# Hybrid decoder layer on one core: turned blocks ahead of the next weights, gates and position table off TensorE

## The chip, the core and the metric

The kernel runs on one core of a Trainium2 chip. Times are device microseconds of one launch. A core has TensorE (PE, with its weight loads as PEld), VectorE (DVE), ScalarE (ACT), GpSimd (POOL) and SyncE (SP), each with its own instruction queue, worked off in order. Here SP issues nearly all DMA transfers. Engines wait for one another by semaphores.

## What is computed

One decoder layer for 256 positions of width 1024, in float32. A combined projection feeds an mLSTM branch (4 heads of 256), an attention branch (8 heads of 128 with a T5 table of relative positions) and two gates; both branches are projected, gated, added and projected again, and a gated MLP with a short convolution follows. Each half ends in a LayerNorm.

```python
def hybrid_mixer(x, w_in, b_in, conv_qk, mlstm_norm, rel_bias, w_branch_a, w_branch_b, w_out):
    proj = jnp.einsum("bsd,dn->bsn", x, w_in) + b_in
    q_m, k_m, v_m, o_m, i_m, f_m, q_b, k_b, v_b, g_a, g_b = _split_cols(proj, SPLIT_SIZES)
    qk = jax.nn.silu(causal_dwconv(jnp.concatenate([q_m, k_m], axis=-1), conv_qk))
    ...
    h_m = mlstm_chunkwise(...)            # i_m, f_m: 4 gates each per position
    y_a = sigmoid(o_m) * head_norm(h_m, mlstm_norm)
    h_b = moba_attention(..., rel_bias)   # 256 positions are one block: plain causal softmax
    merged = sigmoid(g_a) * (y_a @ w_branch_a) + sigmoid(g_b) * (y_b @ w_branch_b)
    return merged @ w_out

x = layer_norm(ALPHA * x + hybrid_mixer(x), ln1_g, ln1_b)
x = layer_norm(ALPHA * x + conv_gated_mlp(x), ln2_g, ln2_b)
```

## The kernel before, in words

All weights stream from HBM in chunks of 1 MB (128 x 2048 floats), in the order that `chunk_order` gives. Each matmul of the reference is three matmuls: every operand is split into a high and a low part (`split_into`, L92 to L95: ScalarE casts to `wh`, VectorE subtracts to `wl`), and high x high, low x high and high x low are summed in PSUM (`mm3`). So a chunk is 48 matmuls on TensorE, and beside it a split of 2048 columns on ScalarE and VectorE, and one transfer on SP.

The order on each engine is the order in which the program is written. The loop over chunks `s` in `run` does, for each: `elem_work(s)`, the element work that waited for the chunk before (`evac`), side work (`side_elem`) and in between the split of chunk s+2; then `load(s + 5)`, a transfer into one of three `raw` buffers, which waits until VectorE has split the chunk that was there; then the chunk's matmuls and side work of TensorE (`side_pe`). `self.mixed[s]` is a function that sets the order of the element work of one step.

The first 32 chunks after the first four come in 4 groups of 8 (qm, qb, km, kb, vm, vb, ga, gb). A group holds one mLSTM head and two attention heads. Beside its chunks run its scores (pss, psl), softmax weights (`lg`), the mLSTM output (psn, then `yt`) and the product of softmax weights and values (pso); `b` is the group's first chunk, and the offsets below count from it. Softmax weights and `yt` have to be turned (transposed) for the products that follow. Groups 0 to 2 do it without TensorE: VectorE turns blocks of 32x32 (`turn`, L658), SP writes them to HBM (`turn_out`, L663, tile `flip`) and reads them back in four transfers (`turn_in`, L671), each read after the write has landed. Write and reads of a block stand in steps of their own, behind the weights of the step before:

```python
self.mixed[b + 7] = lambda w: [lambda: out(0), ...] + w + [..., lambda: dve_t(1)]
self.mixed[b + 8] = lambda w: [lambda: back(0), lambda: out(1), el_n2] + w + [dve_y]
wrap(9, lambda w: [lambda: back(1), lambda: out(2)] + w + [lambda: el_t(0)])
wrap(10, lambda w: [lambda: back(2), lambda: el_t(1)] + w)
```

`el_t` splits the turned softmax weights into `pth`, `ptl`, `ptf`; `el_y` and `el_o` make the halves `yah`, `yal` and `ybh`, `ybl` of the branch inputs. The last group turns on TensorE against an identity (pst for softmax weights, psy for `yt`). After the groups come the branch chunks wa (which read yah, yal) and wb (ybh, ybl), in the order wa, wb, wa, wb, ..., then wo, and the MLP.

TensorE also makes three small things at the start: the table of relative positions (ps_rel, a one-hot product, L567), the turn of the input and forget gates from positions on partitions to positions in a row (ps_gt, L596), where VectorE scans along them, and the turn back of two results (ps_gc, L634).

Of the kernel before, what the change touches and what calls it, by code (L numbers as in the profile page):

```python
# [18 lines left out]
P = 128  # L19
# [25 lines left out]
def chunk_order():  # L45
# [4 lines left out]
    for c in range(4):  # L50
        order += [("wa", c), ("wb", c)]
# [21 lines left out]
class Kernel:  # L73
# [106 lines left out]
    def run(self):  # L180
# [32 lines left out]
        rel = xp.tile([2 * NB, 8], F32, name="rel")  # L213
        onehot = xp.tile([2 * NB, S], F32, name="onehot")
# [39 lines left out]
        twice = (2, NB)  # L254
        small = [(vec, self.vec_d), (ident, self.ident_d)]
        for t, d in ((rel, self.rel_d.unsqueeze(0).to_broadcast([*twice, 8])),
                     (onehot, self.onehot_d[:, 0:S].unsqueeze(0).to_broadcast([*twice, S]))):
            small.append((t, d))
# [21 lines left out]
        both = xp.tile([2 * NB, 8], F32R, name="relhl")  # L280
        oneh = self.ybl.rearrange("p k s -> p (k s)")[0:2 * NB, 0:S]

        def rel_split():
            nc.scalar.copy(both, rel)
            nc.scalar.copy(oneh, onehot)
            nc.vector.tensor_sub(both[NB:], rel[NB:], both[NB:].bitcast(F32))
        self.step_o(whl, bo)
        for s in range(4, 9):
            if s == 7:
                self.split(4)  # L290
            self.load(s)
            if s < 6:
                for _ in range(2):
                    dma(*small.pop(0))
# [36 lines left out]
        self.rel_bias_expand(both, oneh, rel_split)  # L331
        self.gates_schedule(bif)
        for gi in range(NG):
            self.group_schedule(gi)

# [3 lines left out]
                      for i, (m, n) in enumerate(((1, 3), (1, 3), (2, 2)))] for g in range(NG - 1)]  # L339
# [7 lines left out]
        for f in [self.gate_sums] + self.o_sums:  # L347
            f()
        self.split(5)
        for s, (kind, i) in list(enumerate(self.order))[4:]:  # L350
# [3 lines left out]
            if s == first["wa"]:  # L354
# [21 lines left out]
            self.elem_work(s, [] if late else self.split_parts(s + 2))  # L376
# [184 lines left out]
    def rel_bias_expand(self, rel, onehot, split):  # L561
        nc = self.nc
        st = {}

        def pe():
            st["ps"] = ps = self.ps_side([8, S], "ps_rel")
            nc.tensor.matmul(ps, rel, onehot, start=True, stop=True)  # L567

        def elem():
            ev = self.xp.tile([8, LTOE], F32, name="ev")  # L570
            nc.vector.tensor_scalar(ev[:, P:LTOE], self.backward(st["ps"]), 1.0 / ATT_SCALE, None, op0=ALU.mult)
            nc.vector.memset(ev[:, 0:P], NEG)
            nc.gpsimd.dma_start(self.table, ev)
            self.load_band(0)
        self.side_elem.setdefault(4, []).append(split)
        self.mixed[4] = lambda w: w[-1:] + w[:-1]
        self.side_pe.setdefault(4, []).append(pe)
        self.side_elem.setdefault(5, []).append(elem)


    def gates_schedule(self, bif):
        nc, mp = self.nc, self.xp
        st = {}
        v = nc.vector

        def e0():
            gt = mp.tile([P, 2, 8], F32, name="gt")
            for t in range(2):
                v.tensor_add(gt[:, t, :], self.psg[t][:, 256:264], bif)
            st["gt"] = gt  # L590

        def p0():
            ps = self.ps_side([4, 2, S], "ps_gt")
            for w in range(2):
                for t in range(2):
                    nc.tensor.transpose(ps[:, w, t * P:(t + 1) * P], st["gt"][:, t, 4 * w:4 * w + 4], self.ident)  # L596
            st["ps"] = ps

        def e1():
            ps = st["ps"]  # L600
            big = mp.tile([P, KT, S], F32, tag="xraw", name="gates")
            fs, t1, F, G, M, nFM, nM = (big[0:4, k, :] for k in range(7))
            v.tensor_copy(fs, ps[:, 1, :])
            v.scalar_tensor_tensor(t1, fs, -1.0, fs, op0=ALU.mult, op1=ALU.min)
            st["g"] = fs, t1, F, G, M, nFM, nM
# [6 lines left out]
        def e1b():  # L612
            fs, t1, F, G, M, nFM, nM = st["g"]
# [4 lines left out]
        def e1c():  # L618
            fs, t1, F, G, M, nFM, nM = st["g"]
            v.tensor_sub(G, st["ps"][:, 0, :], F)  # L620
            v.tensor_tensor_scan(M, self.ones4[:, S:2 * S], G, 0.0, op0=ALU.max, op1=ALU.max)

        def e1d():
            fs, t1, F, G, M, nFM, nM = st["g"]
            v.tensor_scalar(self.nM[0:4, :], M, -1.0, None, op0=ALU.mult)
            v.scalar_tensor_tensor(nFM, F, -1.0, M, op0=ALU.mult, op1=ALU.subtract)
            st.update(G=G, nFM=nFM)
            nc.sync.dma_start(self.mrows, self.nM[0:4, :])

        def p1():  # L630
            ps = self.ps_side([P, 2, 2, 4], "ps_gc")
            for w, n in enumerate(("G", "nFM")):
                for t in range(2):
                    nc.tensor.transpose(ps[:, w, t, :], st[n][:, t * P:(t + 1) * P], self.ident[0:4, 0:4])  # L634
            st["gc"] = ps

        def e2():
            self.gcol = self.const.tile([P, 2, 4], F32, name="gcol")
            self.floor = self.const.tile([P, 2, 4], F32, name="floor")
            nc.scalar.copy(self.gcol, st["gc"][:, 0])  # L640
            self.floor_exp = lambda: nc.scalar.activation(self.floor, st["gc"][:, 1], AF.Exp)
# [3 lines left out]
        self.side_pe.setdefault(b, []).append(p0)  # L645
# [733 lines left out]
```

## Time and profile before

| | us |
|---|---|
| three runs | 481.77, 482.19, 483.7; median 482.19 |
| the profiled execution: its time, its span | 483.66, 482.0 |
| TensorE, VectorE, ScalarE, POOL busy | 473.4, 368.1, 309.9, 18.8 |
| mean granted clock of TensorE | 0.997 |
| bytes moved by DMA | 96.64 MB, mean 201 GB/s |

In the rows below, L148 is line 148 of the kernel; `out<-in` names the tiles; in a timeline the first number is the start from the span's beginning, the second the duration, both in us, and brackets tell the idle time of the engine ahead of the instruction and what ended it. Matmuls overlap: what one costs is the distance from its start to the next start, not its duration.

### The profile page before, as it was taken

The numbers are of one execution on the slowest core, as the hardware profiler recorded it, in microseconds if no ns is written. First come the engines' busy times: TensorE is split into PE (matmuls) and PEld (weight loads), VectorE is DVE, ScalarE is ACT, GpSimd is POOL, SyncE is SP. The second block draws the span as 40 slices with busy tenths as digits, with TensorE's granted clock in tenths as the row PEclk, the third lists the DMA queues.
The fourth block names the chain that finished last, engine by engine and source line by source line (L and its number), as shares of the span: only waits on it lengthen the run. The fifth ranks groups of instructions, "written<-read, shape, count | busy, mean of one in ns | idle before, by whom it ended". The sixth has DMA issues, their size and how long they took to land.

```text
span 482.0 us, 9466 instructions
## 1 busy us (share of the span) xinstructions
PE 473.4 (98%) x3803; PEld 457.1 (95%) x3803; DVE 368.1 (76%) x647; ACT 309.9 (64%) x543; POOL 18.8 (4%) x42
## 2 busy tenths in 40 slices
PE   8999999999999999999999999999999999999994
PEld 5999999999999999998999999999999999999984
DVE  4887978787768786885766798988768767768876
ACT  5679777777768775977754622767456544556871
POOL 0301001000100010001000001000000000000000
PEclk9999999999999999999999999999999999999998
DMA  7995647754875477544944490827454555456202
GB/s 231 317 333 152 251 176 237 241 191 175 247 234 187 175 244 237 186 176 165 354 181 175 175 349 37 307 97 262 176 195 169 221 201 182 175 194 227 99 0 89
DMA packets 27387, 96.64 MB, mean 201 GB/s; under 512 B 9201, under 2 KB 14013, under 8 KB 18125
## 3 DMA queue, kind: packets, MB, share of 16 engines
q1 hardware_dynamic: 26110, 91.79, 54.2%
q0 software_dynamic: 1232, 4.24, 2.8%
q8 instruction: 30, 0.49, 0.4%
q14 instruction: 15, 0.12, 0.1%
HBM read 92.99 MB, written 3.03 MB: 199 GB/s over the span
## 4 chain that ended last, share of the span: by engine, by line
PE 89%; ACT 4%; DVE 4%; DMA 1%; issue 0%; SPq 0%; DVEq 0%; ACTq 0%
PE ps_up L148 25%; PE ffn L148 13%; PE ps_wb L148 5%; PE mix L148 5%; PE ps_qb L148 5%; PE ps_qm L148 5%; PE ps_km L148 4%; PE ps_wa L148 4%; PE ps_ga L148 3%; PE ps_kb L148 3%; PE ps_vm L148 3%; PE ps_gb L148 3%; PE ps_vb L148 3%; DVE wl L95 2%; ACT wh L94 2%; PE ps_o0a L436 1%
## 5 line engine op out<-in xcount | busy, mean ns | idle before, releaser
L95 DVE TENSOR_TENSOR wl<-raw,wh 128x1024 fp32r<-128x1024 f32 (+4 forms) x147 | 180.2, 1263 | 30.3 <-ACT wh L94 26.6
L94 ACT CAST wh<-raw 128x1024 fp32r<-128x1024 f32 (+4 forms) x147 | 151.9, 1079 | 8.3 <-DMA raw<-in_wst_dram 4.5
L148 PE MATMUL ps_up<-x1h,wl 128*128 128x256 f32 x320 | 88.5, 276 | 0.0
L148 PE MATMUL ps_up<-x1h,wh 128*128 128x256 f32 x320 | 88.4, 276 | 0.0
L148 PE MATMUL ps_up<-x1l,wh 128*128 128x256 f32 x320 | 88.4, 276 | 0.0
L148 PEld LDWEIGHTS ps_up<-x1l,wh 128*128 128x128 f32 x320 | 60.1, 188 | 0.4
L148 PEld LDWEIGHTS ps_up<-x1h,wh 128*128 128x128 f32 x320 | 60.1, 188 | 0.3
L148 PEld LDWEIGHTS ps_up<-x1h,wl 128*128 128x128 f32 x320 | 60.1, 188 | 0.0
L1150 DVE SCALAR_TENSOR_TENSOR cu<-ps_up,vec,cu 128x255 f32<-128x255 f32 (+1 forms) x80 | 33.0, 475 | 20.1 <-ACT cu L1146 20.1
L148 PE MATMUL ffn<-wh,hl 128*128 128x512 f32 (+2 forms) x94 | 35.5, 378 | 0.0
L148 PE MATMUL ffn<-wl,hh 128*128 128x512 f32 (+2 forms) x94 | 35.4, 377 | 0.0
L148 PE MATMUL ffn<-wh,hh 128*128 128x512 f32 (+2 forms) x94 | 35.3, 375 | 0.0
L94 ACT CAST hh<-cu 128x256 fp32r<-128x256 f32 x22 | 8.9, 407 | 40.4 <-DVE cu L1161 40.4
L1146 ACT ACTIVATE cu<-ps_up,vec 128x256 f32<-128x256 f32 x40 | 16.7, 469 | 22.0 <-PE ps_up L148 22.0
L148 PEld LDWEIGHTS ffn<-wh,hl 128*128 128x128 f32 x94 | 17.7, 188 | 3.2
L148 PEld LDWEIGHTS ffn<-wl,hh 128*128 128x128 f32 x94 | 17.7, 188 | 3.1
L148 PEld LDWEIGHTS ffn<-wh,hh 128*128 128x128 f32 x94 | 17.7, 188 | 3.0
L148 PE MATMUL ps_wa<-yal,wh 128*128 128x256 f32 x64 | 18.2, 284 | 0.5 <-DVE yal L803 0.4
L148 PE MATMUL ps_wa<-yah,wh 128*128 128x256 f32 x64 | 18.2, 284 | 0.0
L148 PE MATMUL ps_wb<-ybh,wh 128*128 128x256 f32 x64 | 18.0, 281 | 0.0
L148 PE MATMUL ps_wb<-ybl,wh 128*128 128x256 f32 x64 | 18.0, 281 | 0.0
L148 PE MATMUL ps_wb<-ybh,wl 128*128 128x256 f32 x64 | 18.0, 281 | 0.0
(354 smaller groups left out, 1444.9 us busy)
## 6 DMA issues: line engine op xcount, KB each, us to landing
raw<-in_wst_dram SPq DMA_DIRECT2D x72, 1024.0 KB, 4.9
raw<-in_wst_dram SPq DMA_DIRECT2D x10, 512.0 KB, 6.4
raw<-in_wst_dram SPq DMA_DIRECT2D x8, 256.0 KB, 4.8
lnrow<-in_rows_dram POOLq DMA_DIRECT2D x4, 512.0 KB, 7.0
flip<-turn SPq DMA_DIRECT2D x6, 192.0 KB, 4.4
lg<-flip SPq DMA_DIRECT2D x24, 48.0 KB, 5.2
xraw<-in_xt_dram SPq DMA_DIRECT2D x8, 128.0 KB, 2.6
toe<-table POOLq DMA_DIRECT2D x4, 256.0 KB, 3.9
```

The lines of the kernel that those rows point to most:

```text
L94: self.nc.scalar.copy(wh, raw)
L95: self.nc.vector.tensor_sub(wl, raw, wh.bitcast(F32))
L148: self.nc.tensor.matmul(ps, a[i], b[i], start=start and i == 0, stop=stop and i == 2)
L436: mm(ps[t], x[:, k, t * P:(t + 1) * P], w, start=start and k == 0, stop=stop and k == KT - 1)
L1146: act.activation(cu[:, j, :], ps[:, j, :], AF.Copy, scale=tap(2, j))
L1150: v.scalar_tensor_tensor(cu[:, j, o:], ps[:, j, :S - o], tap(t, j), cu[:, j, o:], op0=ALU.mult, op1=ALU.add)
```

## The change

It has five parts.

1. Write and reads of a turned block are issued together, in the step in which VectorE turns it (`turn` now holds all three), so on SP they stand ahead of that step's weights, and the reads ahead of the next weights. `el_t` comes two steps after the turn, and pso, `el_o` and `el_y` one step earlier than before.
2. The last group's softmax weights go the same way instead of over TensorE; its `yt` still goes over TensorE (psy). Its pso comes after the first wa chunk; `el_y` stands at the head of its step, with half of a weight split (`self.kept`) behind it.
3. The branch chunks come by pairs: wa, wa, wb, wb.
4. The gates are turned by VectorE (32x32 blocks) and put in place by POOL copies; results go back the same way. The exponential of `floor` is taken in place.
5. The table of relative positions is written by POOL, bucket by bucket, from 8 rows; the one-hot input is no longer loaded. One product per group for `scl` moves to POOL.

TensorE at the first chunk of the first group (qm, and after it qb), before:

```order
L148 MATMUL ps_qm_455<-xtl,wh_371 128x256
L148 MATMUL ps_qm_455<-xth,wl_372 128x256
L567 MATMUL ps_rel<-ybl,relhl 8x256
L596 MATMUL ps_gt<-ident,gt 4x128 x4
L148 MATMUL ps_qb_544<-xth,wh_436 128x256
L148 MATMUL ps_qb_544<-xtl,wh_436 128x256
```

and now:

```order
L148 MATMUL ps_qm_479<-xtl,wh_368 128x256
L148 MATMUL ps_qm_479<-xth,wl_369 128x256
L148 MATMUL ps_qb_554<-xth,wh_463 128x256
L148 MATMUL ps_qb_554<-xtl,wh_463 128x256
L148 MATMUL ps_qb_554<-xth,wl_464 128x256
```

The five small matmuls are gone; ps_gc and the six of pst go in the same way.

SP from the second block of the first group on (raw: weights; lg, yt: turned blocks that come back), before:

```order
L671 DMA lg_901<-flip_420 32x4x96 x4
L663 DMA flip_421<-turn 128x384
L89 DMA raw_1106<-in_wst_dram 128x2048
L671 DMA lg_997<-flip_421 32x4x96 x4
L663 DMA flip_422<-turn 128x2x256
L89 DMA raw_1184<-in_wst_dram 128x2048
L671 DMA yt_1008<-flip_422 32x8x64 x4
L89 DMA raw_1254<-in_wst_dram 128x2048
```

and now:

```order
L644 DMA flip_418<-turn 128x384
L648 DMA lg_1010<-flip_418 32x4x96 x4
L89 DMA raw_1055<-in_wst_dram 128x2048
L644 DMA flip_419<-turn 128x2x256
L648 DMA yt_1021<-flip_419 32x8x64 x4
L89 DMA raw_1127<-in_wst_dram 128x2048
L89 DMA raw_1200<-in_wst_dram 128x2048
```

A block's reads stood one transfer of weights behind its write; now they follow it, and SP waits for the write's landing in front of the weights.

ScalarE from the last group's turned weights to the first wa chunk, before:

```order
L94 CAST pth_886<-pst_0_2941 128x256
L863 COPY ptf_888<-pst_0_2941 128x128
L771 ACTIVATE yt_2863<-yt_2863,scl_2862 128x256 x2
L94 CAST pth_889<-pst_1_2945 128x256
L863 COPY ptf_891<-pst_1_2945 128x128
L551 ACTIVATE sga<-ps_ga_2892,vec 128x256 x2
L94 CAST wh_2949<-raw_2688 128x1024 x2
L551 ACTIVATE sgb<-ps_gb_2968,vec 128x256 x2
L802 ACTIVATE yah<-psy_3017,vec 128x256 x2
L883 ACTIVATE ybh<-pso_3022,vec 128x256 x2
```

and now:

```order
L743 ACTIVATE yt_2879<-yt_2879,scl_2878 128x256 x2
L94 CAST pth_898<-lg_2770 128x256
L815 COPY ptf_900<-lg_2770 128x128
L542 ACTIVATE sga<-ps_ga_2916,vec 128x256 x2
L94 CAST wh_2965<-raw_2697 128x1024
L765 ACTIVATE yah<-psy_3027,vec 128x256 x2
L94 CAST wh_2965<-raw_2697 128x1024
L94 CAST pth_901<-lg_2868 128x256
L815 COPY ptf_903<-lg_2868 128x128
L542 ACTIVATE sgb<-ps_gb_2978,vec 128x256 x2
```

The yah pair moved ahead of one cast and of sgb; the second turned block moved behind it.

```diff
 def chunk_order():
...
-    for c in range(4):
-        order += [("wa", c), ("wb", c)]
+    for c in (0, 2):
+        order += [("wa", c), ("wa", c + 1), ("wb", c), ("wb", c + 1)]
...
-            if s == first["wa"]:
+            if s == first["wa"] + 1:
                 self.elem_work(s)
...
+            parts = [] if late else self.split_parts(s + 2)
+            if s == first["wa"] - 1:
+                self.kept, parts = parts[-1], parts[:-1]
+            self.elem_work(s, parts)
             self.load(s + 5)
...
+    def rel_bias_expand(self, rel):
+        g = self.nc.gpsimd
+        ev = self.xp.tile([8, LTOE], F32, name="ev")
+        g.memset(ev[:, 0:P], NEG)
+        bucket = _buckets(np.arange(S))
+        one = int(np.argmax(bucket[1:] == bucket[:-1]))
+        runs = [(0, one, 0)]
+        for b in range(one, NB):
+            d = np.flatnonzero(bucket == b)
+            runs.append((int(d[0]), int(d[-1]) + 1, b))
+        for lo, hi, b in runs:
+            src = rel[:, b:b + 1].to_broadcast([8, hi - lo]) if lo else rel[:, 0:hi]
+            g.tensor_scalar(ev[:, P + lo:P + hi], src, 1.0 / ATT_SCALE, None, op0=ALU.mult)
+        g.dma_start(self.table, ev)
+        self.load_band(0)
...
         def e0():
-            gt = mp.tile([P, 2, 8], F32, name="gt")
+            big = mp.tile([P, KT, S], F32, tag="xraw", name="gates")
+            g.memset(big[:, 7, :], 0.0)
+            g.memset(big[0:32, 0:6:5, :], 0.0)
+            gt, gx = big[:, 7, 0:P], big[:, 7, P:2 * P]
...
+            v.transpose(gx, gt)
+            for j in range(4):
+                src = gx[32 * j:32 * j + 4, :].rearrange("p (t w c) -> p w t c", t=2, w=2)
+                dst = big[0:4, 0:4:3, :].rearrange("p w (t j c) -> p w t j c", t=2, j=4)[:, :, :, j, :]
+                g.tensor_copy(dst, src)
-        def p0():
...
-                    nc.tensor.transpose(ps[:, w, t * P:(t + 1) * P], st["gt"][:, t, 4 * w:4 * w + 4], self.ident)
...
-        def p1():
...
+        def e1e():
+            big = st["big"]
+            for w, k in enumerate((0, 5)):
+                v.transpose(big[0:32, 1 + w, :], big[0:32, k, :])
+            cols = self.const.tile([P, 2, 2, 4], F32, name="gcol")
+            for j in range(4):
+                src = big[0:32, 1:3, :].rearrange("p w (t j c) -> p w t j c", t=2, j=4)[:, :, :, j, 0:4]
+                g.tensor_copy(cols[32 * j:32 * j + 32], src)
...
+    def turn(self, t, d):
+        m, _, f = d.shape
+        n, w = t.shape[1], t.shape[1] // m
+        tmp = self.ap.tile([P, 4 * P], F32, tag="turn", name="turn", bufs=2)[:, 0:n * P]
+        for k in range(m):
+            self.nc.vector.transpose(tmp[:, k * f:(k + 1) * f].rearrange("p (b c i) -> p c b i", b=4, i=32),
+                                     t[:, k * w:(k + 1) * w].rearrange("p c (b i) -> p c b i", b=4))
+        self.nc.sync.dma_start(d.rearrange("m p f -> p m f"), tmp.rearrange("p (m f) -> p m f", m=m))
         t = t.rearrange("p c s -> p (c s)").rearrange("p (k f) -> p k f", k=4 * m)
         for b in range(4):
             src = d[:, :, b * (f // 4):(b + 1) * (f // 4)].rearrange("m (a j) f -> j m a f", a=4)
             self.nc.sync.dma_start(t[32 * b:32 * b + 32], src.rearrange("j m a f -> j (m a) f"))
...
             nc.gpsimd.tensor_tensor(scl, scl, self.mhalf, op=ALU.pow)
+            nc.gpsimd.tensor_tensor(scl, scl, den, op=ALU.mult)
...
         def el_n2():
-            v.tensor_mul(scl, scl, st["den"])
...
-        if flip:
...
-        at(self.side_pe, 6, lambda: pe_t(0))
-        at(self.side_pe, 6, lambda: pe_t(1))
...
-        self.mixed[b + 7] = lambda w: [lambda: el_t(0), el_n2, lambda: el_t(1)] + w
...
+        at(self.side_elem, 5 + o, lambda: turn(0))
+        self.mixed[b + 6 + o] = lambda w: ([lambda: el_l(1), lambda: el_e(1), el_n1] + w
+                                           + [lambda: el_l2(1), el_n1b, lambda: turn(1)])
+        if last:
+            self.mixed[b + 7] = lambda w: [el_n2, lambda: el_t(0)] + w
+            at(self.side_pe, 7, pe_y)
+            self.mixed[b + 8] = lambda w: [el_y, self.kept, lambda: el_t(1)] + w
+        else:
+            self.mixed[b + 8] = lambda w: [el_n2, lambda: el_t(0), lambda: turn(2)] + w
+            self.mixed[b + 9] = lambda w: w[0:1] + [lambda: el_t(1)] + w[1:]
+            at(self.side_elem, 10, el_y)
+        at(self.side_pe, 8 + o, pe_o)
+        at(self.side_elem, 9 + o, el_o)
```

More of the change, by code (lines that the diff above doesn't have):

```diff
@@ L253, in run @@
         nc.gpsimd.partition_broadcast(self.bvm, brow[:, D:2 * D])
[L254 to L258, printed above, removed]
+        small = [(vec, self.vec_d), (ident, self.ident_d), (rel, self.rel_d.rearrange("b h -> h b"))]
         v3 = [t.rearrange("p (k f) -> p k f", k=KT) for t in whl[3]]
@@ L292, in run @@
             if s < 6:
-                for _ in range(2):
+                for _ in range(2 if s == 4 else 1):
                     dma(*small.pop(0))
@@ L346, in run @@
         first = {k: self.order.index((k, 0)) for k in ("wa", "wo", "up")}
[L347 removed]
+        for f in self.o_sums:
             f()
@@ L558, in step_gb @@
         self.step_gate(s, "gb", g, V_BGB)
[L561 to L578, printed above, removed]
+    def rel_bias_expand(self, rel):
[13 more added lines that the diff above has]
+        self.load_band(0)
     def gates_schedule(self, bif):
@@ L628, in e1d @@
             nc.sync.dma_start(self.mrows, self.nM[0:4, :])
-        def p1():
[L631 to L641, printed above, removed]
+        def e1e():
[6 more added lines that the diff above has]
+                g.tensor_copy(cols[32 * j:32 * j + 32], src)
+            self.gcol = cols[:, 0]
+            self.floor = cols[:, 1]
+            self.floor_exp = lambda: nc.scalar.activation(self.floor, self.floor, AF.Exp)
@@ L671, in turn_in @@
             self.nc.sync.dma_start(t[32 * b:32 * b + 32], src.rearrange("j m a f -> j (m a) f"))
-    def turned(self, t):
-        return t.rearrange("p c s -> p (c s)").rearrange("p (a c i) -> p c a i", a=4, i=32)
     def group_schedule(self, g):
@@ L680, in group_schedule @@
         b = self.start_g[g]
-        flip = g < NG - 1
+        last = g == NG - 1
         def row_m():
@@ L845, in el_l2 @@
                 a.activation(o, o, AF.Copy, scale=sm[:, t:t + 1])
-        def pe_t(i):
-            ps = self.ps_side([P, 3, P], f"pst{g}_{i}")
-            for k in range(3):
-                nc.tensor.transpose(ps[:, k, :], st["p", i][:, k, :], self.ident)
-            st["t", i] = ps
-        def el_t(i):
-            th, tl, tf = self.pt[i]
-            if flip:
-                ps = self.turned(st["p", i])
-                th, tl, tf = (t.rearrange("p c (a i) -> p c a i", a=4) for t in (th, tl, tf.unsqueeze(1)))
-                self.split_into(th, tl, ps[:, 0:2])
-                a.copy(tf, ps[:, 2:3])
-                return
-            ps = st["t", i]
-            self.split_into(th, tl, ps[:, 0:2, :])
-            a.copy(tf, ps[:, 2, :])
+        def el_t(i):
+            ps = st["p", i].rearrange("p c s -> p (c s)").rearrange("p (a c i) -> p c a i", a=4, i=32)
+            th, tl, tf = (t.rearrange("p c (a i) -> p c a i", a=4)
+                          for t in (*self.pt[i][0:2], self.pt[i][2].unsqueeze(1)))
+            self.split_into(th, tl, ps[:, 0:2])
+            a.copy(tf, ps[:, 2:3])
         def pe_o():
```

102 lines of the change are left out of this document (25 added, 77 removed).

## The prediction

> **What bounds the kernel now.** I read the page first, then who waited for whom, then single matmuls in order of time.
>
> The page, parts 1 and 4, and the row of the view of waits in which TensorE waits for the work that this change touches (us in total, times, longest):
>
> ```profile
> span 482.0 us, 9466 instructions
> PE 473.4 (98%) x3803; PEld 457.1 (95%) x3803; DVE 368.1 (76%) x647; ACT 309.9 (64%) x543; POOL 18.8 (4%) x42
> PE 89%; ACT 4%; DVE 4%; DMA 1%; issue 0%; SPq 0%; DVEq 0%; ACTq 0%
> ...
> PE ps_wa L148 <- DVE yal L803: 0.4, 1, 0.4
> ```
>
> TensorE is busy 98% of the span and is 89% of the chain that ended last. Whatever leaves its queue comes off the time one for one, as long as VectorE and ScalarE go on splitting each weight chunk before TensorE comes to it. Whatever leaves another engine is worth nothing by itself.
>
> **The change part by part.** In this part I measure a block on TensorE from the last undisturbed matmul ahead of it to the second one behind it, less the two matmuls that stay (0.11 us from start to start), because the matmuls at a block's edges are also slowed.
>
> (a) Position table and first gate turn (ps_rel, ps_gt), timeline of TensorE (start, us):
>
> ```profile
> 33.59 0.28 PE L148 MATMUL ps_qm<-xth,wl 128*128 128x256 f32 x1
> 33.80 0.28 PE L567 MATMUL ps_rel<-ybl,relhl 64*8 64x256 f32 x1
> 34.01 0.60 PE L596 MATMUL ps_gt<-ident,gt 128*4 128x128 f32 x4
> 34.37 0.37 PE L148 MATMUL ps_qb<-xth,wh 128*128 128x256 f32 x1
> 34.57 0.28 PE L148 MATMUL ps_qb<-xtl,wh 128*128 128x256 f32 x1
> ```
>
> From 33.59 to 34.57 is 0.98; less 2 x 0.11 leaves 0.76. (The second gap, 34.37 to 34.57, is such an edge: 0.20 where 0.11 is usual.)
>
> (b) Second gate turn (ps_gc) and (c) the turns of the last group's softmax weights (pst):
>
> ```profile
> 61.59 0.28 PE L148 MATMUL ps_vb<-wh,xtl 128*128 128x256 f32 x1
> 61.80 0.41 PE L634 MATMUL ps_gc<-ident,gates 4*128 4x4 f32 x4
> ...
> 62.36 0.28 PE L148 MATMUL pss<-qml,kmh 128*128 128x256 f32 x1
> ...
> 215.79 0.28 PE L148 MATMUL ps_ga<-xth,wl 128*128 128x256 f32 x1
> 215.91 0.97 PE L850 MATMUL pst<-ident,lg 128*128 128x128 f32 x6
> ...
> 216.84 0.28 PE L148 MATMUL ps_gb<-xtl,wh 128*128 128x256 f32 x1
> ```
>
> (b) 0.77 - 0.22 = 0.55. (c) 1.05 - 0.22 = 0.83. Together (a) to (c) give 2.14 us. This term is nearly certain.
>
> (d) The first wa chunk waits inside itself for yal of the last group:
>
> ```profile
> 225.72 0.28 PE L148 MATMUL ps_wa<-yah,wl 128*128 128x256 f32 x1
> ...
> 227.73 0.39 PE L148 MATMUL ps_wa<-yal,wh 128*128 128x256 f32 x1
> 227.95 0.28 PE L148 MATMUL ps_wa<-yah,wl 128*128 128x256 f32 x1
> ```
>
> From 225.72 to 227.95 stand six steps; 2.23 - 6 x 0.11 = 1.57 us are lost, though the view of waits names 0.4 of it: a modelled matmul end hides the rest. What is late is seen on ScalarE:
>
> ```profile
> 220.09 0.27 ACT L863 COPY ptf<-pst 128x128 f32<-128x128 f32 x1 [1.54 <-DVE ptl L95]
> 222.80 2.00 ACT L94 CAST wh<-raw 128x1024 fp32r<-128x1024 f32 x2
> 224.69 0.86 ACT L551 ACTIVATE sgb<-ps_gb,vec 128x256 f32<-128x256 f32 x2
> 225.41 0.49 ACT L802 ACTIVATE yah<-psy,vec 128x256 fp32r<-128x256 f32 x1
> 226.68 0.47 ACT L802 ACTIVATE yah<-psy,vec 128x256 fp32r<-128x256 f32 x1 [0.77 <-DVE yal L803]
> ```
>
> The yah pair stands behind a whole weight split and the sgb pair. The change puts it behind half a split: one cast of 1.00 and the 0.86 of sgb leave its front, and the 1.54 spent waiting between two turned blocks goes with pst. The chain yah, yal, yah, yal still runs one by one, from 225.41 until yal lets 227.73 start: 2.3 us. TensorE asks for the first yal of the pair 19 matmuls into the chunk, some 2.2 us after it starts, and for the second three matmuls later; psy, of which yah is made, ends just ahead of the chunk. So with ScalarE and VectorE free at that moment next to nothing is lost, and with the two no earlier than now all 1.57 stay. ScalarE should be earlier, since waits like the 3.9 us one in the next row go with (e). I take 1.2 of 1.57; bounds 0 and 1.57.
>
> (e) Turned blocks. Views: waits, the tile turn, and the timelines of SP and VectorE in the first group:
>
> ```profile
> ACT pth L94 <- DMA lg<-flip: 14.1, 6, 3.9
> ...
> DMA to landing us min/median/max: 2.2/4.4/5.3
> ...
> raw<-in_wst_dram SPq DMA_DIRECT2D x72, 1024.0 KB, 4.9
> ...
> 68.51 0.58 DVE L658 STREAM_TRANSPOSE turn<-lg 128x384 f32<-128x384 f32 x1
> ...
> 75.10 0.58 DVE L658 STREAM_TRANSPOSE turn<-lg 128x384 f32<-128x384 f32 x1
> ...
> 78.80 3.95 SPq L671 DMA_DIRECT2D lg<-flip  x4
> ...
> 84.00 0.35 SPq L89 DMA_DIRECT2D raw<-in_wst_dram  x1
> 87.25 1.74 SPq L671 DMA_DIRECT2D lg<-flip  x4
> ...
> 104.98 0.28 PE L148 MATMUL ps_vb<-wh,xth 128*128 128x256 f32 x1
> ...
> 210.43 2.36 DVE L95 TENSOR_TENSOR wl<-raw,wh 128x1024 fp32r<-128x1024 f32 x2 [1.08 <-ACT wh L94]
> ```
>
> Now SP issues a write as soon as its turn ends, waits until it has landed, issues four reads, and only then the next weights. Walked along the queue of the first group: turn 0 ends at 69.1, its write finds an empty queue (2.2) and lands at 71.3; four reads, 1.7 us as at 87.25, end at 73.0, and the weights behind them leave then. Turn 1 ends at 75.7; its write lies behind that megabyte, takes the median 4.4 and lands at 80.1, the reads end at 81.8, and the next weights leave there. The third write goes out right behind them, lands at 86.5 to 87.1 (4.4 to 5.3), its reads end at 88.8, and the third weights leave at 88.8 instead of 84.00. What waits there is chunk ps_vb of the next group, on TensorE at 104.98 now and 1.3 earlier then, 103.7; its split takes a cast of 1.0 and then two subtractions of 2.36 together, 3.4 us (the second cast runs beside them), so the weights must land by 100.3. Issued at 88.8, with the 4.9 us of the 1024 KB row, they land at 93.7: 6.6 us of cover. TensorE doesn't feel it, and the weights behind them leave when VectorE lets them, as now. In return the reads of a block are out 3.9 to 8.2 us after its turn, and with the least landing of 2.2 it is back after 6 to 10.4; it is asked for two chunks after the turn (2 x 48 matmuls at 0.11, 10.6 us), so that most of the 14.1 us go in which ScalarE waits for flip. VectorE's and ScalarE's lead covered these, so the worth is 0 on TensorE: bounds 0 and the 0.25 that follows.
>
> In the last group yal and ybl of the group before it stand ahead of kbl, and TensorE waits for kbl; they move two chunks ahead:
>
> ```profile
> 202.64 0.36 PE L148 MATMUL psl<-kbh,qbh 128*128 128x256 f32 x1
> 203.00 0.39 PE L148 MATMUL psl<-kbl,qbh 128*128 128x256 f32 x1
> ```
>
> The step of 0.36 is 0.11 where nothing waits: 0.25. The two turns that the last group gets (0.58 each on VectorE) fall into idle time ahead of its splits, such as the 1.08 at 210.43: 0; without that cover they would cost 1.16 at most.
>
> (f) wa, wa, wb, wb: the same matmuls in another order. pso of the last group moves behind the first wa, so the second turned block has a chunk more to come back, and its own result is asked for two chunks later: 0; if the block were late even so, ScalarE's longest such wait so far, 3.9, is the most.
>
> (g) Gates and table on POOL: 4 copies and 17 small tensor_scalar from about 29 us on. The nearest rows are POOL's tensor_scalar of 0.28 and cast of 0.45, so 5.9 to 9.5 us, done by 40; the table is first read for the logits whose turned weights leave at 68.51. That alone is hidden, as is the one product for scl that goes from VectorE to POOL in each group. SP has one small transfer fewer (the one-hot rows), ahead of weights that wait for VectorE anyway: 0. But POOL's reading disturbs VectorE:
>
> ```profile
> 12.66 1.30 POOL L252 PARTITION_BROADCAST bo<-sga  x1 [10.57 <-DMA sga<-in_rows_dram]
> 13.84 1.69 POOL L253 PARTITION_BROADCAST bvm<-sga  x1
> 12.82 1.55 DVE L95 TENSOR_TENSOR wl<-raw,wh 128x512 fp32r<-128x512 f32 x1 [0.16 <-ACT wh L94]
> 29.88 2.35 DVE L95 TENSOR_TENSOR wl<-raw,wh 128x1024 fp32r<-128x1024 f32 x2
> 474.79 0.28 POOL L1269 TENSOR_SCALAR few<-few 128x1 f32<-128x1 f32 x1 [4.18 <-ACT junk L1265]
> ```
>
> The subtraction of 512 columns takes 1.55 beside the broadcasts; at the rate of the row at 29.88 (2.35 for four times as many) it takes 0.6. VectorE lost a little over half of the time that POOL was reading; half of 5.9 to 9.5 is 3 to 4.8 us, spread over some 10 us. The tightest split there starts at 29.88 and ends at 32.2; TensorE asks for that chunk (ps_qb) at 34.37 less 0.76, 33.6: 1.4 us of cover. I take 0, since about a third of the loss falls before that point; bounds 0 and -2.
>
> The Trainium skill, "SBUF — State Buffer" (SBUF: two separate sides), calls the port pair of VectorE and GpSimd an exclusive lock for an instruction with two SBUF inputs. The rows above go its way, half of the time. By that rule every subtraction beside these pieces may be held, against my 0; the second rival below is this mechanism, priced from the rows.
>
> **Sum.** 2.14 + 1.2 + 0.25 = 3.6 us; I round down to 3.4 for a pso that may wait a little behind wa. The profiled execution took 483.66 (span 482.0, 1.66 around it), so 480.3 by its own account. It stands near the upper end of the three runs (481.77 to 483.7); from the median 482.19 the same gain gives 478.8.
>
> **Rivals.** First, the stall at wa stays (ScalarE is bound by its own program order in the last group, as the 2.00 us casts standing back to back suggest): gain 2.1 to 2.4, 479.9. Against it: the 14.1 us of waits that go. Second, POOL slows VectorE early: 1 to 2 us lost at the second and third chunk, gain 1.9, 480.3. Third, slower: SP's held queue. If each write takes more than the longest 5.3, each four reads the 3.95 seen above, and the reads' small pieces slow the megabytes beside them, the three holds of a group add up and its third weights land after 100.3; each microsecond after that is paid in each of three groups. At 2.5 us late: 3 x 2.5 - 3.4 = +4.1, 486.3. Against it: 6.6 us of cover.
>
> **How the numbers follow.** Forecast 0.62, first rival 0.18, second 0.12, third 0.08. Half a percent, 2.4 us, is about what a measurement here can tell from no change. Faster: nearly all of the forecast (0.56 of 0.62), a third of the first rival, a little of the second: 0.64. Slower: 0.08. Same: 0.28. The range goes from 477.6 (all bounds favourable: 4.0, and a run 0.6 low) to 481.2, which takes in the first two rivals and leaves out the third.
>
> **What would show it.** Right: no pst, ps_gt, ps_gc, ps_rel on TensorE; the six steps in the first wa chunk at 0.7 to 1.1 us instead of 2.23; no wait of pth for flip above 1 us; no new gap between the chunks of a group. Wrong: TensorE waiting for wl with raw behind it (third rival), or VectorE subtractions over 1.5 us between 29 and 39 us with TensorE idle there (second).

## The result

| | before | changed |
|---|---|---|
| median, us (14 executions each, side by side) | 482.26 (479.96 to 484.62) | 478.74 (478.0 to 479.85) |
| ratio, changed to before | | 0.9925, 95% interval 0.9904 to 0.9946 |
| the profiled execution, us (span) | 483.66 (482.0) | 478.69 (476.7) |

The change makes the kernel 3.5 us (0.75%) faster, and the forecast of 478.8 us is met to 0.1. Two things in the table ask for more than a nod. The executions of the kernel before lie 4.7 us apart, those of the changed one 1.9. And the two profiled executions differ by 5.0 us, 1.5 more than the medians.

The page of the changed kernel (span, busy times, the chain that ended last), and the rows of its view of waits that name the turned blocks (us in total, times, longest):

```profile
span 476.7 us, 9493 instructions
PE 469.3 (98%) x3788; PEld 454.8 (95%) x3788; DVE 368.1 (77%) x644; ACT 309.7 (65%) x540; POOL 37.4 (8%) x74
...
PE 98%; DVE 0%; ACT 0%; DVEq 0%; issue 0%; ACTq 0%
```

```profile
ACT yah L765 <- DMA yt<-flip: 11.0, 3, 4.4
...
ACT pth L94 <- DMA lg<-flip: 1.1, 1, 1.1
```

TensorE was 89% of the chain and is 98% of it: behind the start nothing holds it up. (That much the kernel before reaches too, in an execution without the long stall: 98% in its second profile, E0 below.) ScalarE's wait for lg, 14.1 us, has shrunk to 1.1. A wait for yt has come in its place, 11.0 us, and TensorE doesn't feel that one.

The first wa chunk of the changed kernel, on TensorE (start, us; the rows are six steps apart) and on ScalarE:

```profile
222.40 0.28 PE L148 MATMUL ps_wa<-yah,wl 128*128 128x256 f32 x1
...
223.08 0.28 PE L148 MATMUL ps_wa<-yah,wl 128*128 128x256 f32 x1
```

```profile
220.66 0.48 ACT L765 ACTIVATE yah<-psy,vec 128x256 fp32r<-128x256 f32 x1 [2.04 <-PE psy L752]
221.69 0.47 ACT L765 ACTIVATE yah<-psy,vec 128x256 fp32r<-128x256 f32 x1 [0.55 <-DVE yal L766]
```

Six steps take 0.68 us where they took 2.23. ScalarE now stands waiting 2.04 us for psy, where before it came late.

The second half of the difference is found by laying the chunks behind it side by side. The first rows of two neighbouring chunks, before (one chunk of 48 matmuls lies between) and changed (two chunks, 96 matmuls):

```profile
230.89 0.28 PE L148 MATMUL ps_wb<-ybh,wh 128*128 128x256 f32 x1
...
236.55 0.28 PE L148 MATMUL ps_wa<-yah,wh 128*128 128x256 f32 x1
```

```profile
232.53 0.28 PE L148 MATMUL ps_wb<-ybh,wh 128*128 128x256 f32 x1
...
243.41 0.28 PE L148 MATMUL ps_wa<-yah,wh 128*128 128x256 f32 x1
```

5.66 us over 48 is 118 ns from start to start, 10.88 over 96 is 113. In the profiled execution of before all seven chunks behind the stall run at 118: 7 x 48 x 4.4 ns = 1.5 us that I had not seen. Nothing waits in them, and the granted clock is 1.00 in both kernels.

So the two profiles differ as follows (us): work taken off TensorE and the psl wait, from the first chunk of the first group up to psy, 2.29 (forecast 2.14 + 0.25); stall in the first wa chunk 1.55 (forecast 1.2); the 118 ns steps 1.47 (forecast nothing); 5.3 in all, which is the difference of the spans. (Two small things cancel: the changed kernel comes to that first chunk 0.13 later, and the rest of the first wa chunk is 0.1 faster in it.) Only 3.5 of it is in the medians, so some of what the one profile of before shows is not there in every execution. The experiments went after that.

### The profile page after: what moved, and what is told of

It is laid out like the page before. It is cut to its first block, busy times and chain, and to the rows that moved or that the text cites. A ratio compares the mean times of both kernels' runs of the same rounds, so it can differ in the third digit from the quotient of the medians.

```text
span 476.7 us, 9493 instructions
## 1 busy us (share of the span) xinstructions
PE 469.3 (98%) x3788; PEld 454.8 (95%) x3788; DVE 368.1 (77%) x644; ACT 309.7 (65%) x540; POOL 37.4 (8%) x74
## 4 chain that ended last, share of the span: by engine, by line
PE 98%; DVE 0%; ACT 0%; DVEq 0%; issue 0%; ACTq 0%
PE ps_up L148 25%; PE ffn L148 13%; PE ps_ga L148 5%; PE ps_kb L148 5%; PE ps_vm L148 5%; PE mix L148 5%; PE ps_km L148 5%; PE ps_gb L148 5%; PE ps_wa L148 5%; PE ps_vb L148 5%; PE ps_wb L148 5%; PE ps_qm L148 5%; PE ps_qb L148 5%; PE ps_o0a L427 1%; PE ps_o0b L427 1%; PE psn L148 1%
## 5 line engine op out<-in xcount | busy, mean ns | idle before, releaser
L990 POOL TENSOR_TENSOR rs<-rs,mhalf 128x1 f32<-128x1 f32 x3 | 2.1, 700 | 230.2 <-DVE rs L989 230.2
L148 PE MATMUL ps_ga<-xth,wh 128*128 128x256 f32 x64 | 18.0, 281 | 0.0
L148 PE MATMUL mix<-wh,mgh 128*128 128x256 f32 x64 | 17.8, 279 | 0.0
L148 PE MATMUL ps_kb<-xth,wl 128*128 128x256 f32 x64 | 17.7, 277 | 0.0
```

The lines of the kernel that those rows point to most:

```text
L148: self.nc.tensor.matmul(ps, a[i], b[i], start=start and i == 0, stop=stop and i == 2)
L990: nc.gpsimd.tensor_tensor(st["rs"], st["rs"], self.mhalf[:, 0:1], op=ALU.pow)
```

## The experiments

Each was timed in turn with the kernel before, except for the second profile of it. The medians of before beside them were 481.93 (E1 to E4), 480.6 (E5 to E7) and 481.53 (E8 to E10); all 104 executions of before together lie between 479.8 and 485.1 us, 40 of them below 480.7.

### E0: the kernel before, a second profile

> The kernel before, unchanged, for a second profile: its times lie between 479.8 and 484.8 us. Theory of the waits that come and go (the stall in the first wa chunk depends on how long the turned blocks of the third group were under way, and the 118 ns steps come behind a short wait of TensorE, in some executions): an execution near 480.0 has no stall over 0.2 us there and 113 ns in all eight branch chunks; one of 482 or more has a stall, the 118 ns, or the granted clock at 0.5 behind it. Theory of the prediction (the stall of 1.57 us belongs to the program): the stall is 1.4 to 1.7 us again, whatever the time.

482.81 us (span 481.0). The second block of the third group on ScalarE, the yah pair, and TensorE in the first wa chunk:

```profile
186.35 0.41 ACT L94 CAST pth<-lg 128x256 fp32r<-128x256 f32 x1 [2.86 <-DMA lg<-flip]
...
223.55 0.50 ACT L802 ACTIVATE yah<-psy,vec 128x256 fp32r<-128x256 f32 x1
```

```profile
225.87 0.38 PE L148 MATMUL ps_wa<-yal,wh 128*128 128x256 f32 x1
226.09 0.28 PE L148 MATMUL ps_wa<-yah,wl 128*128 128x256 f32 x1
...
229.03 0.28 PE L148 MATMUL ps_wb<-ybh,wh 128*128 128x256 f32 x1
...
234.69 0.28 PE L148 MATMUL ps_wa<-yah,wh 128*128 128x256 f32 x1
```

The same rows of the first profile of before:

```profile
188.24 0.41 ACT L94 CAST pth<-lg 128x256 fp32r<-128x256 f32 x1 [3.93 <-DMA lg<-flip]
```

The stall is one step of 0.22, 0.1 us lost instead of 1.57: its size doesn't belong to the program. Where it came from can be read off. In the first profile the block came back at 188.24, here at 186.35, 1.89 earlier; the yah pair started at 225.41 there and starts at 223.55 here, 1.86 earlier. From that block up to the pair, 37 us further on, the rows of VectorE and ScalarE name only waits for each other (up to 2.2 us), none for a DMA or for TensorE, so a late block of the third group stays late all the way. The 118 ns steps are there all the same: one wait of 0.1 us is ahead of them (229.03 to 234.69 is 5.66 again), and they go on through mix (23.3 us from its first row to its last instead of 22.6).

### E1: the yah/yal pair ahead (part d alone)

```
+            if s == first["wa"] - 1:
+                self.kept, parts = parts[-1], parts[:-1]
...
-        at(self.side_elem, 8, el_y)
+        self.mixed[b + 8] = lambda w: [el_y, self.kept] + w
```

> The kernel before, with one part of the change: in the last group the yah/yal pair stands ahead of the sgb pair and of the second half of the split instead of behind both. Theory of the prediction (the stall of 1.57 us inside the first wa chunk is only the wait for the second yal): the six steps take 0.7 to 1.1 us instead of 2.23, and the whole gains 1.1 to 1.6 us, about 481.0 beside 482.2. Theory of the slower rate (after the stall the 336 matmuls of the other seven wa and wb chunks run at 118 ns start to start instead of 113, 1.5 us in all, and the stall sets that rate off): the seven chunks come down from 5.65 to 5.44 each too, and the gain is 2.6 to 3.1 us, about 479.3. Rival (ScalarE is too late in the last group in any case, since it still waits 1.5 us for the turned blocks): the stall stays above 1 us and the gain is under 0.5.

480.34 us (479.96 to 481.86); ratio to before 0.9982, 95% interval 0.9965 to 0.9999. ScalarE in the last group:

```profile
222.36 0.47 ACT L805 ACTIVATE yah<-psy,vec 128x256 fp32r<-128x256 f32 x1 [0.58 <-PE psy L792]
```

The pair waits for psy now, TensorE doesn't wait for the pair, and all eight chunks run at 113 ns. The kernel isn't faster than the fastest executions of before; those above 482 us are gone. So part (d) takes no fixed 1.2 us off: it takes off what the late blocks cost when they are late. In this set that is 1.6 us between the medians, 0.9 by the ratio.

### E2: the changed kernel with the pair behind again

```
-            self.mixed[b + 8] = lambda w: [el_y, self.kept, lambda: el_t(1)] + w
+            self.mixed[b + 8] = lambda w: [self.kept, lambda: el_t(1)] + w + [el_y]
```

> The changed kernel, with the yah/yal pair of the last group put back behind the whole split and the sgb pair. Theory of the prediction: the stall returns in part, 0.4 to 1.6 us, and nothing else: 479.1 to 480.3. Theory that the stall sets off the slower rate: if the stall is there, the seven chunks behind it take 5.65 again, and the loss is 1.5 us more, 480.6 to 481.8. If the rate stays at 113 ns with a stall of over 0.5 us in the chunk, the stall isn't its cause.

479.47 us (478.35 to 483.46); ratio to before 0.9978, 0.9948 to 1.0007. Seven executions lie between 478.3 and 479.6, five between 481.3 and 483.5. The profiled one is of the second sort (482.52). The mean granted clock is 0.993 or 0.994 in the four slowest and 0.996 or more in the others. ScalarE, TensorE, and the busy times of a window (the number behind POOL's is the granted clock):

```profile
221.90 0.41 ACT L94 CAST pth<-lg 128x256 fp32r<-128x256 f32 x1 [1.17 <-DMA lg<-flip]
```

```profile
222.06 0.28 PE L148 MATMUL ps_wa<-yah,wl 128*128 128x256 f32 x1
223.66 0.38 PE L148 MATMUL ps_wa<-yah,wh 128*128 128x256 f32 x1 [1.32 <-ACT yah L765]
...
225.43 0.28 PE L148 MATMUL ps_wa<-yah,wl 128*128 128x256 f32 x1
```

```profile
226.00:229.40 3.40, 3.40 (x18) 3.40 (x17) 1.96 (x2) 2.43 (x3) 0.00 (x0) 0.50 0.52 186
```

A block that comes back late stands ahead of the pair again, and TensorE loses 2.7 us in six steps (3.37 less 6 x 0.11). Then the granted clock falls to 0.50 for 3.4 us, the steps last 213 ns, and another 1.6 us are lost. The theory that a stall always brings the 118 ns steps fell here: behind all this the matmuls run at 113.

### E3: the order wa, wa, wb, wb alone

> The kernel before, with the branch chunks in the order wa, wa, wb, wb and nothing else changed. Theory of the prediction: no difference (482.2, within 0.5). Theory that the order of the chunks (alternating left and right operands from yah and ybh) makes the slower rate: the seven chunks run at 113 ns with the stall still there, 1.5 us faster, 480.7. Theory that the stall makes it: stall and 118 ns both stay.

481.55 us (480.0 to 484.7); ratio 1.0004, 0.998 to 1.0028. No difference, as forecast for part (f). In the profiled execution the stall is one step of 0.22, and the steps behind it are 113 ns.

### E4: gates and table off TensorE, alone

The edit takes out ps_rel, ps_gt and ps_gc and puts in the new forms of both functions, as in the change.

> The kernel before, with the gates and the position table off TensorE and nothing else changed (no ps_rel, ps_gt, ps_gc). Theory of the prediction: 0.76 and 0.55 us less on TensorE, 1.3 us faster, 480.9. Rival (GpSimd's pieces slow VectorE's subtractions, and TensorE waits for a split in the first group): gain under 0.5, with a gap of TensorE between 29 and 50 us, or a wait of the first exponential of the weights for the columns.

483.79 us (480.7 to 484.94); ratio 1.0042, 1.0014 to 1.0069. Neither 1.3 us faster nor the same: slower. TensorE in the last group and in the first wa chunk of its profiled execution (482.93):

```profile
202.38 0.36 PE L148 MATMUL psl<-kbh,qbh 128*128 128x256 f32 x1
202.91 0.39 PE L148 MATMUL psl<-kbl,qbh 128*128 128x256 f32 x1 [0.17 <-DVE kbl L502]
```

```profile
225.63 0.28 PE L148 MATMUL ps_wa<-yah,wl 128*128 128x256 f32 x1
...
226.61 0.38 PE L148 MATMUL ps_wa<-yal,wh 128*128 128x256 f32 x1 [0.36 <-DVE yal L782]
```

The three blocks are gone from TensorE, and it waits instead: 0.5 us at psl, 0.2 at psn of the second group, 1.5 in the first wa chunk. The last is the lateness of E0 again, on ScalarE:

```profile
188.08 0.41 ACT L94 CAST pth<-lg 128x256 fp32r<-128x256 f32 x1 [3.44 <-DMA lg<-flip]
...
225.32 0.50 ACT L781 ACTIVATE yah<-psy,vec 128x256 fp32r<-128x256 f32 x1
```

From the block to the pair are 37.2 us, as in both profiles of before (and in E3, 187.22 to 224.39). Two more losses have nothing to do with turned blocks. TensorE waits 0.6 us at the start (ps_o2a, 14.3) for a subtraction that takes 1.38 us beside the partition broadcasts. And from the last matmul to the end 7.2 us pass, where they are 6.4 in the kernel before (7.2 in E6 too). That this edit causes either is not shown. VectorE's subtractions beside GpSimd's new pieces take 2.40, 2.35 and 2.21 us where they took 2.35, 2.35 and 2.21, so the work moved to GpSimd isn't the cause. The executions of 484 to 485 were not profiled; what they lose beyond this is not shown.

### E5: the turned blocks of the first three groups ahead, alone

```
...
-            self.mixed[b + 8] = lambda w: [lambda: back(0), lambda: out(1), el_n2] + w + [dve_y]
+            self.mixed[b + 8] = lambda w: [el_n2, lambda: el_t(0), lambda: trip(2)] + w    # trip: turn, out, back
...
```

> The kernel before, with the order of the turned blocks of the first three groups alone (write and reads right behind the turn, ahead of the next weights); the last group, the gates, the table and the branch chunks as before. Theory of the prediction: worth 0 on TensorE but for 0.25; the stall in the first wa chunk stays, 482.0. Theory of the inherited lateness (the second block of the third group comes back late, ScalarE waits 3.9 us for it, VectorE and ScalarE have no slack left after it and arrive at the wa chunk 2 us late, which is the stall): no wait of pth for flip over 1.5 us, VectorE's splits behind that place 2 us earlier, the stall in the wa chunk under 0.4 us in nearly every execution, and the times close to the lowest of the kernel before: 480.0 to 480.6, with little spread.

481.28 us (480.04 to 484.6); ratio 1.0009, 0.9988 to 1.0031. TensorE in the first wa chunk:

```profile
225.93 0.35 PE L148 MATMUL ps_wa<-yal,wh 128*128 128x256 f32 x1
226.11 0.28 PE L148 MATMUL ps_wa<-yah,wl 128*128 128x256 f32 x1
226.23 0.28 PE L148 MATMUL ps_wa<-yah,wh 128*128 128x256 f32 x1
```

The wait of pth for flip is gone (the view names none), and the stall is 0.07 us (one step of 0.18). But that was enough: from the very next step on the matmuls are 118 ns apart, through all eight chunks. The lateness theory named a stall under 0.4, which came, but E0 has one of 0.1 without this change; and it is wrong about the time. Alone this part gains nothing that can be measured, because the pair still arrives just when TensorE asks for it. ScalarE shows why (the first row from the view of waits: us in total, times, longest):

```profile
ACT yah L802 <- DMA yt<-flip: 8.0, 3, 3.0
...
188.20 0.91 ACT L802 ACTIVATE yah<-yt,vec 128x256 fp32r<-128x256 f32 x2 [3.02 <-DMA yt<-flip]
```

The wait has moved from lg to yt, the third block of the same group. It ends at 188.20, and the pair starts at 223.57, as in E0 (223.55).

### E6: gates off TensorE and the pair ahead

> The kernel before, with the gates and the table off TensorE (which alone came out at 483.8) and the yah/yal pair of the last group ahead (which alone came out at 480.3). Theory of the stall (the 1.3 us that TensorE loses in work made it arrive earlier at an unchanged yal, so that the stall grew and the granted clock fell to a half behind it): with the pair ahead the 1.3 us come through, 479.0, little spread. Rival (GpSimd's pieces or the table are what costs time in the gates kernel): 482 or more.

482.67 us (480.56 to 484.83); ratio 1.0034, 1.0008 to 1.0059. My theory fell: with the pair ahead the gates bring nothing either. TensorE at the end of the first group's blocks:

```profile
92.07 0.28 PE L857 MATMUL pso<-pth,vbl 128*128 128x256 f32 x1
92.75 0.38 PE L854 MATMUL pso<-pth,vbh 128*128 128x256 f32 x1 [0.40 <-ACT pth L94]
```

TensorE, 1.3 us earlier, now waits inside the groups: 0.57 us here for a block turned by way of DRAM, and shorter at psn in three groups. Behind the one at psn of the third group four chunks run at 118 ns, and behind one in the first wa chunk all that follow.

### E7: a later pair in the changed kernel

Four or ten copies on ScalarE ahead of the pair, each of 256 columns of psy; nothing reads them.

```
+            def late():
+                for _ in range(4):        # 10 in the second kernel
+                    a.copy(st["wt"][:, 0:2, :].rearrange("p t c -> p (t c)"), st["psy"][:, 0, :])
+            self.mixed[b + 8] = lambda w: [late, el_y, self.kept, lambda: el_t(1)] + w
```

> The changed kernel, with four copies of 256 columns on ScalarE (0.37 to 0.49 us each, 1.6 us together) between psy and the yah/yal pair of the last group; nothing reads their result. Theory that only the wait costs: a stall of 1.5 to 1.9 us in the first wa chunk and as much lost, 480.4. Theory of the clock (a stretch of about 3.4 us with TensorE mostly idle may bring the granted clock to 0.5 for as long, which costs another 1.7): most executions at 480.4, some at 482.1.

> The same with ten copies, 4 us. Theory that only the wait costs: 4.0 to 4.4 us lost, 482.9. Theory of the clock: the granted clock falls to 0.5 behind the stall in every execution, the matmuls go from 113 to 213 ns for 3.4 us, and 5.7 to 6.1 us are lost, 484.6.

Four: 479.91 us (479.47 to 480.73); ratio 0.9974, 0.9954 to 0.9994. Ten: 483.56 us (482.04 to 486.45); ratio 1.0052, 1.0028 to 1.0076. TensorE with four:

```profile
222.47 0.28 PE L148 MATMUL ps_wa<-yah,wl 128*128 128x256 f32 x1
...
224.51 0.28 PE L148 MATMUL ps_wa<-yah,wl 128*128 128x256 f32 x1
```

Six steps take 2.04 us, 1.4 lost, and behind them come 113 ns and the full clock: 1.2 us against 478.74, the wait and no more. With ten, windows of the profiled execution (486.01):

```profile
222.00:225.50 3.50, 1.09 (x7) 0.71 (x5) 0.48 (x1) 2.79 (x8) 0.00 (x0) 0.93 0.62 260
225.50:231.80 6.30, 6.30 (x28) 6.00 (x28) 4.41 (x6) 6.24 (x10) 0.00 (x0) 0.50 0.36 134
```

and TensorE at the stall:

```profile
225.04 0.58 PE L148 MATMUL ps_wa<-yah,wh 128*128 128x256 f32 x1 [2.41 <-ACT yah L765]
```

2.6 us of stall, then more than 6 us at half the clock, then 118 ns steps in all seven chunks. Other executions of this kernel lose as little as 3.3 us, so "in every execution" was too much. Which of the two they escape isn't profiled, but the mean granted clock points to the half clock: 0.996 and 0.997 in the two fastest executions (482.04 and 482.2), 0.990 to 0.995 in the other ten.

### E8: SP's queue held longer

```
...
+        for e in more:                       # two fresh buffers in DRAM, for the third block only
+            self.nc.sync.dma_start(e, tmp)
+            self.nc.sync.dma_start(tmp, e)
```

> The changed kernel, with two more round trips of the third block (128x512 out and back into the turn buffer, some 4 to 5 us each) between the four reads of yt and the next weights, in the first three groups; nobody reads their result. Theory of the prediction (6.6 us between the landing of the third weights and the point at which TensorE feels it, 4.7 by the walk as it came out): the weights leave 8 to 10 us later, land 3.5 to 5.5 us too late in each of the three groups, and 10 to 16 us are lost, 489 to 495. Rival (SP's hold has far more cover, or the weights behind catch up): under 2 us lost. The third rival of the prediction, slower by SP's held queue, is bounded by it either way.

491.6 us (490.05 to 497.29); ratio 1.0228, 1.0158 to 1.0298: 12.9 more than the changed kernel. SP's queue and TensorE in the second group:

```profile
97.51 8.80 SPq L89 DMA_DIRECT2D raw<-in_wst_dram  x4
```

```profile
103.61 0.39 PE L148 MATMUL ps_vb<-wh,xth 128*128 128x256 f32 x1
104.87 0.38 PE L148 MATMUL ps_vb<-wl,xth 128*128 128x256 f32 x1 [0.87 <-DVE wl L95]
```

The third weights leave at 97.51, 6.8 us later than in the changed kernel, and TensorE loses 1.3 us at the chunk that I had named. 1.3 less would have cost nothing there: 96.2. The forecast had them in time if they left by 95.4 (6.6 us of cover behind 88.8). The third rival is a real mechanism, then, and the cover that spoke against it was rightly sized. The price is higher than a microsecond for each late one: the weights leave 2.1 us behind those 95.4, and the second group loses 4.7 against the changed kernel, 1.3 at this chunk and 1.8 at psn behind it, where TensorE waits for ScalarE (sph).

### E9 and E10: gates and turned blocks; and the pair as well

> The kernel before, with the gates and the table off TensorE (alone: 483.8) and the turned blocks of the first three groups ahead of the weights, the yah/yal pair as before. Theory that the turned blocks bound the gates kernel (TensorE, 1.3 us earlier, waits for what VectorE and ScalarE bring late): most of the 1.3 us come through, 479.0 to 479.8, or 1.5 more in executions with a short wait for the pair and the 118 ns. Rival (what slows the gates kernel is GpSimd's work): 482 or more.

> As the one before, and the yah/yal pair ahead as well: everything of the change but the last group's softmax weights and the order of the branch chunks. Theory of the turned blocks: no wait of TensorE behind the start, 113 ns throughout, the whole gain of the gates, 480.0 less 1.3: 478.7, spread under 1.5 us. Rival (GpSimd's work): 482 or more.

E9 479.87 us (479.28 to 483.96), ratio 0.9974, 0.9949 to 1.0; E10 479.55 us (478.99 to 484.36), ratio 0.9958, 0.9929 to 0.9986. GpSimd does the same work here as in E4 and E6, so it isn't what made those slow. E9 is E4 with the turned blocks ahead, and the median goes from 483.79 to 479.87. The two were timed beside different executions of before, whose medians differ by 0.4. In E9 and E10 TensorE waits at no yal and at no kbl; what is left in the groups are waits of about a quarter of a microsecond, at psn and pso of the first. E10 is 0.9 slower than I expected. Its profile, laid beside that of E1 less 1.3, is 0.7 too long: 0.5 at those two places, 0.15 at the start, the rest at the end. Its spread is 5.4 us, not under 1.5: two of its twelve executions took 481.3 and 484.4, and they were not profiled. Of the change E10 lacks the last group's softmax weights (pst is still on TensorE), the pairs of chunks and the product for scl; it is 0.8 behind the changed kernel, which fits term (c), 0.83.

## Why the prediction came out, point by point

**Work taken off TensorE (a, b, c): right.** 2.14 and the 0.25 at psl were forecast, 2.39 together; 2.29 were measured up to psy. What the step "nearly certain" left out is that such a gain needs VectorE, ScalarE and the blocks on their way to be that much earlier too. E4 took 1.3 us of it and ended slower.

**The stall in the first wa chunk (d): the size right, the cause half right.** "I take 1.2 of 1.57": 1.55 in the profile. The pair's place behind a split and sgb is part of it (E1, E2). But I priced the stall as a property of the program, out of one execution. In E0 it is 0.1 us, and in the fastest executions of before there is no room for one: the lowest time with the pair ahead, 479.96, is also that of before, 480.02 in the same set.

**The turned blocks (e): the step that failed.** "VectorE's and ScalarE's lead covered these, so the worth is 0 on TensorE." For the first two groups the lead did cover them. In the third group the wait of up to 3.9 us uses it up, and in the last one VectorE and ScalarE wait only for each other, so nothing wins it back: 1.89 us at the block is 1.86 us at the yah pair (E0 beside the first profile). The longest of the waits that make up the 14.1 us and the 1.57 us that I put into another term are one chain. And once TensorE is 1.3 us earlier, the order of the blocks is worth 3.9 us between medians (E4 to E9); of the 3.1 us between those two profiles 1.1 lie at the start and at the end, where no turned block acts, and 2.0 between. On its own the order is worth nothing measurable (E5). Nor did the wait go: the sign "no wait of pth for flip above 1 us" was just missed (1.1), and 11.0 us of waiting for yt came, which the prediction didn't have.

The walk along SP's queue in the changed kernel:

```profile
83.18 0.39 SPq L644 DMA_DIRECT2D flip<-turn  x1
88.82 1.80 SPq L648 DMA_DIRECT2D yt<-flip  x4
90.72 0.87 SPq L89 DMA_DIRECT2D raw<-in_wst_dram  x2
```

The third write is away for 5.6 us beside a megabyte, 0.3 more than the longest I had, and the weights leave at 90.72, not 88.8. No chunk waits for it. (My walk has a slip: 81.8 and 4.4 give 86.2, not 86.5; the 88.8 comes from the other bound.)

**Pairs (f): right,** 1.0004 (E3).

**GpSimd (g): right in effect, wrong in detail.**

```profile
29.27 1.26 POOL L588 COPY gates<-gates 4x128 f32<-4x128 f32 x4 [6.33 <-DVE gates L584]
...
38.53 7.68 POOL L565 TENSOR_SCALAR ev<-rel 8x16 f32<-8x16 f32 x17 [7.84 <-issue]
46.51 0.73 POOL L566 DMA_DIRECT2D table<-ev  x1 [0.30 <-POOL ev L565]
```

The 21 pieces take 8.9 us, within my 5.9 to 9.5, but GpSimd stands still for 7.84 us between the two kinds, and the table is done at 46.2 instead of 40. The logits first use it at 65.2. That the sum fits is luck. By shapes (us busy and mean ns; then the idle time ahead):

```profile
L565 POOL TENSOR_SCALAR ev<-rel 8x16 f32<-8x16 f32 x1 | 2.7, 2666 | 7.8 <-issue 7.8
L565 POOL TENSOR_SCALAR ev<-rel 8x3 f32<-8x3 f32 x3 | 0.7, 220 | 0.2
L565 POOL TENSOR_SCALAR ev<-rel 8x143 f32<-8x143 f32 x1 | 0.6, 569 | 0.1
```

Fifteen of the 17 pieces take 0.21 to 0.25 us, less than my 0.28 to 0.45; the first takes 2.67. VectorE's pair of subtractions that runs beside that first one:

```profile
38.85 2.21 DVE L95 TENSOR_TENSOR wl<-raw,wh 128x1024 fp32r<-128x1024 f32 x2
```

It takes 2.21 us, and 2.21 in the kernel before as well. So VectorE loses nothing here (beside most of the later pieces it is idle), and the second rival has nothing to show. It is GpSimd that is held: its piece ends at 41.19, 0.13 behind the pair. My "half of the time that POOL was reading" came from two partition broadcasts, and there, too, one engine was held whole: the next subtraction in that profile, of 256 columns from 14.29 on, takes 1.38 us where its like take 0.42, and ends 0.13 behind the second broadcast. That agrees with the exclusive port pair of the Trainium skill, "SBUF — State Buffer" (SBUF: two separate sides), which one of the two engines gets while the other is blocked.

**The sum: right by two errors that cancel.** I added 3.6 and rounded to 3.4; the two profiles differ by 5.3. The 1.5 us of 118 ns steps stood in the trace I had (chunks of 5.66 us where others take 5.44), and I didn't read it. On the other side the profiled execution was one of the slower ones, and I took its whole stall off the median of the others. That the forecast is met to 0.1 is luck to that extent. Lowest against lowest the gain is 1.8 us over all sets (479.8 and 478.0) and 2.0 in the first. The other 1.5 to 1.7 of the 3.5 I put down to what an average execution of before loses to late blocks and to what follows them; the two profiles of it show such losses, the average is not shown. The half clock of E2 is not among them: all 90 executions of before whose clock is on record beside E1 to E10 have a mean of 0.996 or more. Some of the spread arises earlier: in the 14 profiles the first group starts between 28.0 and 29.1 us.

## What to carry to other kernels

A stall in a profile is one draw: if it hangs on a transfer's round trip, take a second profile, or look at the spread of the times, before it goes into a sum. Lateness of an engine off the critical path isn't harmless because the engine catches up in other groups; follow it forward to the place where that engine has no idle time left, and price it there. And an engine relieved of work only gets the gain if its suppliers are early by as much; here the relief alone made the kernel slower, and the part that looked worthless made it count.

## What the runs showed of the hardware

**Two rates of the same matmuls.** Rows of 128x256 in fp32r run 113 or 118 ns apart, at a granted clock of 1.00. The slower rate set in right behind a short wait of TensorE, 0.07 to 1.57 us (both profiles of before, E5, E6), or behind a spell at half the clock (E7 with ten copies). It then held for hundreds of matmuls, over 60 us in E0. It didn't follow every wait: behind 1.5 us in E4 and 1.4 in E7 with four copies the rate stayed at 113, and of two waits of the same 0.1 us it came behind that in E0 and not behind that in E3. It ended with the first row of mix in the first profile of before, but not in E0. What decides it stays open; no run here was made to break it off.

**The granted clock.** Behind 2.7 us lost in 3.4 (E2) it fell to 0.50 for 3.4 us, behind 2.6 us in one piece (E7, ten copies) for more than 6; behind 1.4 and 1.6 us it stayed. The spell of 3.4 us in E2 costs 1.6. The Trainium skill, "TensorE: Matmul & The Clock Gate" (The HAM clock gate), describes a free-running window of some 3.4 us, and half rate after one in which TensorE was idle. The length of the spells agrees with it; but here TensorE was not idle for a whole window: a few matmuls ran within it.

**Small instructions on GpSimd.** In the changed kernel pieces of 8x2 to 8x14 take 0.21 to 0.25 us each, one of 8x143 takes 0.57. A stop of 7.84 us lies ahead of the first of them (7.12 in E4), for which the profile names no releaser.

**VectorE and GpSimd.** One can hold the other until it is done. In the nine profiles of kernels with the new table, one piece of the table takes 1.9 to 2.7 us and ends 0.08 to 0.13 us behind the pair of subtractions beside it; and one of four copies of 32x16 takes 5.4 us, where two take 0.19, and ends 0.06 behind a row of VectorE instructions that follow one another without a pause. There GpSimd waits, over several instructions of VectorE; at the partition broadcasts it is VectorE that waits.
